# Post-LayerNorm shift (x += ab) as an accumulating DMA instead of a VectorE add, in a four-layer hybrid diffusion step

## The chip, the cores and the metric

The kernel runs on one core of one Trainium2 chip. The metric is the device time of one execution in microseconds. All matrix work is done by TensorE (PE). VectorE (DVE), ScalarE (ACT) and GpSimd (POOL) prepare operands, empty PSUM and normalise. SyncE (SP) and GpSimd issue the transfers, which all run on the same 16 DMA engines.

## The reference

640 tokens (128 of context, 512 latent) of width 1024 pass through four layers. A layer has a token mixer (gated linear attention, Conformer convolution, short convolution, and attention again) and a squared-ReLU MLP. After each of these eight sublayers the residual stream is normalised and the next one reads a modulated copy:

```python
xs = layer_norm(ALPHA * xs + ms[2] * os_, ln_g[l, 0], ln_b[l, 0])
fs = sqrelu_mlp(modulate(xs, ms[3], ms[4]), ff_w1[l], ff_w2[l])
xs = layer_norm(ALPHA * xs + ms[5] * fs, ln_g[l, 1], ln_b[l, 1])
```

`layer_norm` is (x − mean) / std · g + b. What is stored for the next residual addition is ALPHA times that, so the kernel keeps x · (ALPHA·g) + (ALPHA·b).

## The kernel before

The residual stream stays in SBUF as five tiles `x[t]` of 128 tokens by 1024 values in fp32. Every fp32 product is made of three matmuls: each weight tile of 512 KB is loaded by SP into one of 5 buffers `st`, cast by ScalarE to `whi` (L107), and VectorE makes the rest `wlo` (L108); 6 buffers of each hold weights ahead of PE. PSUM gives the mixers' and the MLP's products five banks, two named `mm` and three named `mx` (`bank`). PE needs a free bank for each pass, and ScalarE or VectorE frees one by copying it out.

`mm1` makes products with weights stationary. Of the first four weights it runs the left 384 columns first and then the right 256 columns one by one. After each it calls `evac`, which in the MLP is two ReLUs out of PSUM on ScalarE (L1159, L1160), a square on VectorE (L1162), a cast on ScalarE (L1163) and a subtraction on VectorE (L1164). Then it runs one entry of the list `self.later`. `mm2` makes the products that go back to the residual stream.

The last `mm2` of a sublayer ends in `norm_epi`, which calls `ln` for each token tile: statistics, normalisation in place, and 6.2 us of matmul time later `rest`, which transposes x, modulates it into `hT` (the operand of the next sublayer, L397 and L398) and puts the closure `affine` on `self.later`. `affine` is the stored g and b: x is multiplied by `ag` and `ab` (named `abr` in the trace) is added. Neither is needed until the next sublayer's residual addition (L205), tens of microseconds later. `issue_after(self.mark.ins)` holds the two behind the latest `hT` on VectorE's queue.

There are seven such groups of five tiles, one behind every sublayer but the last: in the trace their first multiplications start at 391.9 (in the MLP of layer 0), 856.9 (Conformer), 1099.5 (MLP of layer 1), 1565.1 (short convolution), 1793.4 (MLP of layer 2), 2283.9 (attention of layer 3) and 2585.2 us (MLP of layer 3).

`ag` and `ab` have one buffer each. After the group is done `load_ln` loads the next norm's vectors into them on GpSimd's DMA queue (L371), and ScalarE multiplies them by ALPHA in place (L373), except for the last norm. In the attention layers other tiles (`za`, `wgb`) take over the buffers (`lower`, L575).

The order of PE's instructions is that of the program (`manual_schedule`). The other engines' queues are ordered at build time by a planner with its own costs (`schedule_with_timeline_sim=True`). On the chip each queue runs strictly in that order, and an instruction that waits holds up all behind it on its engine.

Of the kernel before, what the change touches and what calls it, by code (L numbers as in the profile page):

```python
# [11 lines left out]
AL = mybir.AluOpType  # L12
# [54 lines left out]
class Net:  # L67
# [352 lines left out]
    def ln(self, t, nxt, last):  # L420
        nc, x = self.nc, self.x[t]
        mv = self.stats(x[:, :512], x[:, 512:], LN_EPS)
        if not last:
            nc.vector.tensor_scalar(
                out=x[:, :512], in0=x[:, :512], scalar1=mv[:, 0:1], scalar2=mv[:, 3:4], op0=AL.subtract, op1=AL.mult)
            nc.scalar.activation(x[:, 512:], x[:, 512:], AF.Identity, bias=mv[:, 4:5], scale=mv[:, 3:4])
            ag, ab = self.ag, self.ab

            def affine():
                with self.tc.issue_after(self.mark.ins):  # L430
                    nc.vector.tensor_tensor(out=x, in0=x, in1=ag, op=AL.mult)
                    nc.vector.tensor_tensor(out=x, in0=x, in1=ab, op=AL.add)

            def rest():
                self.modulated(t, nxt)
                self.later.append(affine)

            self.after(LN_GAP, rest)
            return
        dst = self.out["y_prompt"] if t == 0 else self.out["y_sample"][(t - 1) * 128:t * 128, :]  # L440
        for n in range(2):
            c = slice(n * 512, (n + 1) * 512)
            nc.scalar.activation(x[:, c], x[:, c], AF.Identity, bias=mv[:, 4:5], scale=mv[:, 3:4])
            nc.vector.tensor_tensor(out=x[:, c], in0=x[:, c], in1=self.ag[:, c], op=AL.mult)
            nc.vector.tensor_tensor(out=x[:, c], in0=x[:, c], in1=self.ab[:, c], op=AL.add)
            nc.sync.dma_start(dst[:, c], x[:, c])
# [853 lines left out]
```

## Time and profile before

| | |
|---|---|
| median of 3 runs | 3029.47 us (3028.68 to 3032.02) |
| profiled execution | 3029.77 us, of it the span from first to last instruction 3028.0 us |
| busy, share of the span | PE 98%, VectorE 61%, ScalarE 33%, GpSimd 5% |
| DMA | 350.28 MB, mean 116 GB/s |
| mean granted TensorE clock | 0.995 of full speed |

The profiled execution lies 0.3 us above the median. The 1.8 us between its time and its span lie outside the instructions.

### The profile page before, as it was taken

How to read it: one execution, taken by the hardware profiler on the slowest of the kernel's cores; microseconds unless marked ns; L12 is line 12 of the kernel's file. 1: busy time of each engine (PE TensorE's matmuls, PEld its weight loads, DVE VectorE, ACT ScalarE, POOL GpSimd, SP SyncE). 2: the span in 40 equal slices, each digit the busy share in tenths (PEclk: the TensorE clock that was granted, in tenths of full speed). 3: DMA queues.
4: the chain of work that ended last, by engine and by line, in shares of the span. 5: the costliest groups of instructions: out<-in, count | busy, mean ns of one | idle time of the engine just before them, and what ended most of it. 6: DMA issues, size and time to landing. Idle time of an engine off the chain costs nothing.

```text
span 3028.0 us, 42170 instructions
## 1 busy us (share of the span) xinstructions
PE 2978.6 (98%) x17452; PEld 2620.9 (87%) x17452; DVE 1850.4 (61%) x2737; ACT 999.6 (33%) x1592; POOL 154.5 (5%) x295
## 2 busy tenths in 40 slices
PE   7999999999999899999999999999999999999998
PEld 5888798898888697988999988988988887998997
DVE  4444877767597775775484486774465448644345
ACT  4333442232242341332242142322344434322221
POOL 0000100000010010000010010000010001000000
PEclk9999999999999999999999999999999999999999
DMA  6334244445165334452232133541223212322120
GB/s 247 121 122 157 87 140 150 151 151 173 65 177 135 114 110 156 162 169 93 83 112 77 63 112 112 174 164 67 82 70 121 105 63 86 107 87 73 63 91 36
DMA packets 101792, 350.28 MB, mean 116 GB/s; under 512 B 12940, under 2 KB 18572, under 8 KB 101600
## 3 DMA queue, kind: packets, MB, share of 16 engines
q1 hardware_dynamic: 91888, 317.79, 31.6%
q0 software_dynamic: 9712, 29.80, 3.0%
q8 instruction: 137, 2.24, 0.3%
q14 instruction: 55, 0.45, 0.0%
HBM read 340.29 MB, written 7.24 MB: 115 GB/s over the span
## 4 chain that ended last, share of the span: by engine, by line
PE 95%; DMA 2%; DVE 1%; ACT 1%; issue 1%; POOL 0%; SPq 0%; DVEq 0%; ACTq 0%; POOLq 0%
PE mx L143 23%; PE mm L189 22%; PE mx L189 20%; PE mm L143 19%; PE md L273 1%; PE md L338 1%; PE mx L1004 1%; PE tp L408 1%; PE o L798 1%; PE tp L778 1%; PE tp L725 1%; PE o L764 1%; DMA st<-in_gvr 1%; PE tp L748 1%; PE mm L1004 1%
## 5 line engine op out<-in xcount | busy, mean ns | idle before, releaser
L107 ACT CAST whi<-st 128x1024 fp32r<-128x1024 f32 (+1 forms) x378 | 396.0, 1050 | 1099.0 <-PE mx L189 290.7
L143 PE MATMUL mx<-hT,whi 128*128 128x256 f32 (+1 forms) x3216 | 706.9, 310 | 1.7 <-DVE hT L398 1.5
L108 DVE TENSOR_TENSOR wlo<-st,whi 128x1024 fp32r<-128x1024 f32 (+1 forms) x378 | 459.9, 1221 | 373.7 <-ACT whi L107 368.1
L143 PE MATMUL mm<-hT,whi 128*128 128x384 f32 (+1 forms) x2592 | 566.4, 309 | 1.1 <-DVE hT L398 0.8
L143 PEld LDWEIGHTS mx<-hT,whi 128*128 128x128 f32 x3216 | 541.9, 189 | 5.9 <-DVE hT L398 3.0
L143 PE MATMUL mx<-hT,wlo 128*128 128x384 f32 (+1 forms) x1608 | 497.8, 310 | 0.0
L189 PE MATMUL mx<-whi,act 128*128 128x512 f32 (+1 forms) x1536 | 484.7, 389 | 0.0
L143 PEld LDWEIGHTS mm<-hT,whi 128*128 128x128 f32 x2592 | 434.0, 189 | 5.0 <-DVE hT L398 1.7
L143 PE MATMUL mm<-hT,wlo 128*128 128x256 f32 (+1 forms) x1296 | 399.7, 308 | 0.4 <-DVE wlo L108 0.4
L189 PEld LDWEIGHTS mx<-whi,act 128*128 128x128 f32 x1536 | 287.9, 188 | 61.1 <-issue 1.7
L189 PE MATMUL mm<-whi,act 128*128 128x512 f32 (+1 forms) x1040 | 330.2, 388 | 0.0
L143 PEld LDWEIGHTS mx<-hT,wlo 128*128 128x128 f32 x1608 | 304.4, 189 | 2.5 <-issue 2.5
L189 PE MATMUL mx<-wlo,act 128*128 128x512 f32 (+1 forms) x768 | 299.2, 390 | 0.0
L320 DVE SCALAR_TENSOR_TENSOR acc<-st,cm,acc 128x512 f32<-128x512 f32 x392 | 275.9, 745 | 34.3 <-ACT acc L318 34.0
L189 PE MATMUL mm<-whi,hT 128*128 128x512 f32 x888 | 286.1, 395 | 0.0
L143 PEld LDWEIGHTS mm<-hT,wlo 128*128 128x128 f32 x1296 | 245.2, 189 | 7.8 <-issue 6.7
L189 PEld LDWEIGHTS mm<-whi,act 128*128 128x128 f32 x1040 | 194.8, 188 | 41.2 <-issue 1.7
L189 PE MATMUL mm<-wlo,act 128*128 128x512 f32 (+1 forms) x520 | 202.3, 389 | 0.0
L189 PEld LDWEIGHTS mm<-whi,hT 128*128 128x128 f32 x888 | 165.5, 188 | 31.9
L204 DVE TENSOR_TENSOR mx<-mx,gate 128x512 f32<-128x512 f32 x120 | 83.5, 696 | 162.5 <-PE mx L189 162.3
L189 PE MATMUL mm<-wlo,hT 128*128 128x512 f32 x444 | 177.3, 399 | 0.0
L189 PEld LDWEIGHTS mx<-wlo,act 128*128 128x128 f32 x768 | 144.3, 188 | 36.3 <-issue 7.5
(250 smaller groups left out, 3158.1 us busy)
## 6 DMA issues: line engine op xcount, KB each, us to landing
st<-in_w SPq DMA_DIRECT2D x256, 512.0 KB, 3.6
st<-in_modv SPq DMA_DIRECT2D x112, 512.0 KB, 4.1
st<-in_modw SPq DMA_DIRECT2D x80, 512.0 KB, 4.5
st<-in_gvr SPq DMA_DIRECT2D x32, 512.0 KB, 5.4
st<-in_cpw SPq DMA_DIRECT2D x24, 512.0 KB, 4.8
st<-in_scin SPq DMA_DIRECT2D x24, 512.0 KB, 3.5
ur<-uscr SPq DMA_DIRECT2D x40, 238.0 KB, 5.8
st<-in_gqk SPq DMA_DIRECT2D x16, 512.0 KB, 5.4
```

What stands on the lines that cost most here:

```text
L107: self.nc.scalar.copy(hi[:, :n], src)
L108: self.nc.vector.tensor_tensor(out=lo[:, :n], in0=src, in1=hi[:, :n].bitcast(F32), op=AL.subtract)
L143: self.nc.tensor.matmul(ps[:m, :n], w[a][:, kt * m:(kt + 1) * m], self.hT[:, h, kt, c0:c0 + n], start=(i == 0), stop=(i == 3 * KT - 1),)
L189: self.nc.tensor.matmul(ps, lhs(kt, h, t), s[a][:, c + cols.start:c + cols.stop], start=(i == 0), stop=(i == 3 * nk - 1))
L204: self.nc.vector.tensor_tensor(out=ps, in0=ps, in1=g, op=AL.mult)
L273: nc.tensor.matmul(ps[32 * t:32 * t + 32, :], self.cm[:, kt, :], st[t // 2][:, c:c + 512], start=(kt == 0), stop=(kt == KT - 1),)
L320: nc.vector.scalar_tensor_tensor(out=acc[:, s], in0=w, scalar=c, in1=acc[:, s], op0=AL.mult, op1=AL.add)
L338: nc.tensor.matmul(ps[r:r + 32, :], self.ones, acc[:, s], start=True, stop=True)
L408: nc.tensor.transpose(tp[:, i * 128:(i + 1) * 128], x[:, k * 128:(k + 1) * 128], self.ident)
L725: nc.tensor.matmul(sp[:, i, dd], self.tri[:, 2 + dd], G[:, t0 + i, dd], start=True, stop=True)
L748: nc.tensor.matmul(sc[:, i], Em[i][:, ts], Ep[i][:, ts], start=True, stop=True)
L1004: nc.tensor.matmul(ps[32 * g:32 * g + 32, :5 * GRID], w[:, g, q], ur[i][:, g, :, 4 * q:4 * q + GRID], start=(q == 0), stop=(q == 7))
```

## The change

In `affine` the multiplication stays on VectorE. The addition becomes a DMA that GpSimd issues: it reads the 512 KB of `ab` and accumulates them into `x` in SBUF. It stands outside the `issue_after` block. The program is otherwise the same, and the planner orders the queues anew.

```diff
             def affine():
                 with self.tc.issue_after(self.mark.ins):
                     nc.vector.tensor_tensor(out=x, in0=x, in1=ag, op=AL.mult)
-                    nc.vector.tensor_tensor(out=x, in0=x, in1=ab, op=AL.add)
+                nc.gpsimd.dma_start(x, ab, accum_op=AL.add)
```

## Rows read from the trace of the kernel before

**Rows 1.** The page's head and part 1: busy time, share of the span, instructions.

```profile
span 3028.0 us, 42170 instructions
...
PE 2978.6 (98%) x17452; PEld 2620.9 (87%) x17452; DVE 1850.4 (61%) x2737; ACT 999.6 (33%) x1592; POOL 154.5 (5%) x295
```

**Rows 2.** PE's waits from 60 us on: us in total, times, longest.

```profile
PE mm L1004 <- DMA ur<-uscr: 3.7, 1, 3.7
...
PE mm L143 <- ACT r L1160: 0.4, 1, 0.4
PE mx L143 <- ACT r L1159: 0.2, 1, 0.2
```

**Rows 3.** VectorE's groups of instructions: busy us, mean ns, idle before.

```profile
L432 DVE TENSOR_TENSOR x<-x,abr 128x1024 f32<-128x1024 f32 x35 | 40.5, 1217 | 0.0
```

**Rows 4.** Timeline of VectorE, 386 to 412 us: start, us, instruction.

```profile
391.93 5.76 DVE L431 TENSOR_TENSOR x<-x,ag 128x1024 f32<-128x1024 f32 x5
397.60 5.76 DVE L432 TENSOR_TENSOR x<-x,abr 128x1024 f32<-128x1024 f32 x5
```

**Rows 5.** Timeline of GpSimd, 386 to 412 us.

```profile
397.99 0.62 POOL L371 DMA_DIRECT2D ag<-in_ln_g  x1 [13.54 <-DVE x L431]
403.67 0.53 POOL L371 DMA_DIRECT2D abr<-in_ln_b  x1 [5.06 <-DVE x L432]
```

**Rows 6.** Timeline of ScalarE, 386 to 412 us.

```profile
408.10 1.06 ACT L373 ACTIVATE abr<-abr 128x1024 f32<-128x1024 f32 x1
...
409.68 0.48 ACT L1159 ACTIVATE r<-mx 128x384 f32<-128x384 f32 x1
```

**Rows 7.** Timeline of PE, 408 to 412 us.

```profile
410.22 0.62 PE L143 MATMUL mx<-hT,whi 128*128 128x384 f32 x2 [0.18 <-ACT r L1159]
```

**Rows 8.** DMA issues of the whole span: KB each, median us to landing.

```profile
ur<-uscr SPq DMA_DIRECT2D x40, 238.0 KB, 5.8
...
gate<-gate POOLq DMA_DIRECT2D x16, 512.0 KB, 4.5
...
abr<-in_ln_b POOLq DMA_DIRECT2D x8, 512.0 KB, 4.5
...
gate<-gate POOLq DMA_DIRECT2D x4, 256.0 KB, 3.5
```

**Rows 9.** Timelines of ScalarE in three other groups.

```profile
875.04 1.06 ACT L373 ACTIVATE abr<-abr 128x1024 f32<-128x1024 f32 x1 [1.74 <-DMA abr<-in_ln_b]
...
879.09 0.59 ACT L962 ACTIVATE u<-mx,prm 128x384 f32<-128x384 f32 x1 [2.04 <-PE mx L143]
...
1581.80 1.06 ACT L373 ACTIVATE abr<-abr 128x1024 f32<-128x1024 f32 x1 [0.81 <-DMA abr<-in_ln_b]
...
1589.86 1.05 ACT L107 CAST whi<-st 128x1024 fp32r<-128x1024 f32 x1 [3.16 <-PE mm L143]
...
1809.48 1.05 ACT L373 ACTIVATE abr<-abr 128x1024 f32<-128x1024 f32 x1
```

**Rows 10.** Windows: stretch, busy us of each engine, PE clock, DMA share, GB/s.

```profile
391.00:404.00 13.00, 13.00 (x92) 13.00 (x90) 12.79 (x13) 2.57 (x4) 0.96 (x2) 1.00 0.27 100
...
870.00:890.00 20.00, 20.00 (x157) 19.31 (x159) 16.47 (x20) 7.06 (x13) 0.55 (x1) 1.00 1.00 262
2283.00:2298.00 15.00, 15.00 (x87) 12.61 (x89) 15.00 (x19) 1.99 (x5) 0.00 (x0) 1.00 0.00 0
```

**Rows 11.** Timelines of GpSimd, SP and PE, first convolution of the Conformer.

```profile
870.67 0.55 POOL L985 DMA_DIRECT2D uscr<-u  x1 [0.99 <-DVE u L964]
...
877.75 3.67 SPq L997 DMA_DIRECT2D ur<-uscr  x8
...
888.83 4.51 PE L1004 MATMUL mm<-ur,st 128*32 128x320 f32 x64
```

**Rows 12.** Timeline of ScalarE, attention of layer 3.

```profile
2297.97 0.72 ACT L575 CAST za<-low 98x640 fp32r<-98x640 f32 x1 [7.57 <-DVE x L432]
...
2310.62 1.04 ACT L107 CAST whi<-st 128x1024 fp32r<-128x1024 f32 x1 [8.80 <-DMA st<-in_gqk]
```

## The prediction

> **What bounds the kernel now.** I read the page's busy times first. PE is busy for 2978.6 of 3028.0 us [rows 1], so whatever is taken from another engine is worth only the part of PE's idle time that it ends. Next I read what PE waits for once the opening is past. There are 14 entries between 3.7 us and 0.2 us, and they add up to 22.9 us [rows 2]. Only two of them stand behind an affine group, both of them waits for ScalarE to empty a PSUM bank, 0.4 and 0.2 us. The largest, 3.7 us, is a convolution's transfer 100 us after the nearest group. VectorE is busy for 61%, so its time in the sum bounds nothing.
>
> Then I read the group itself, in the MLP of layer 0. Five multiplications run from 391.93 us, and five additions from 397.60 us to 403.36 us, without a gap [rows 4]. The reader is to see what hangs on their ends. The load of the next `ag` is issued 0.3 us after the last multiplication, that of the next `abr` at 403.67 us, 0.3 us after the last addition [rows 5]. ScalarE scales `abr` at 408.10 us [rows 6], 4.43 us after that issue, as long as such a load takes to land [rows 8]. It stands in the middle of ScalarE's queue: the next PSUM copy (L1159) comes at 409.68 us [rows 6], and PE is already waiting for it at 410.22 us, for 0.18 us [rows 7]. So a chain with no slack leads from the last addition through a transfer and ScalarE to PE. It is hidden only because each piece ends just in time.
>
> **What the change takes away.** 35 additions of 1217 ns, 40.5 us of VectorE [rows 3]. VectorE gets free 5.7 us earlier in each group and squares the ReLUs sooner, which can end the two small waits, 0.6 us in all [rows 2]. I count −0.6 us. No multiplication moves, since each stays behind the same `hT`.
>
> **What it adds on GpSimd.** 35 issues at about the 0.53 us of the `abr` load [rows 5], 19 us on an engine that is busy for 5% [rows 1]. Each waits for one multiplication, and these end 1.14 us apart, so in a group GpSimd is held for about 6 us. In that stretch it otherwise stands waiting for the same multiplications (13.54 us before `ag` [rows 5]). I cost the issues at nothing. Behind them stand the loads of `ag` and `abr`, and in the Conformer the copy `uscr` at 870.67 us [rows 11]. What that costs is priced below.
>
> **What it adds in the wait for `abr`.** The buffer is free when five accumulating transfers have landed, not when five additions have ended. No transfer into SBUF with arithmetic is in the trace, so I bound it. From GpSimd's queue 512 KB land in 4.5 us and 256 KB in 3.5 us [rows 8]. Worked out from these, 512 KB more cost 2.0 us and a transfer's fixed part is 2.5 us. The first accumulate can be issued at 391.93 + 1.22 + 0.3 = 393.4 us.
> - Lower bound: it costs as much as a copy. The last one lands at 393.4 + 2.5 + 5 × 2.0 = 405.9 us, `abr` is issued at 406.2 and scaled at 410.6 us. That is 2.5 us later than now.
> - Upper bound from rows: it reads `x` as well as `ab`, so its traffic counts twice, 4.0 us each. The last one lands at 415.9 us, and `abr` is scaled 12.5 us late.
> - I take 2.7 us each, a third of the way up: the writing is that of a copy and only the reading doubles. Last landing 409.4 us, `abr` scaled 6.0 us late.
>
> The DMA engines themselves have room there: their share is 0.27 from 391 to 404 us [rows 10].
>
> The Trainium skill (DMA: Bandwidth & Descriptors, Rules for kernel authors) says that an accumulating DMA reads its destination and writes it later. No run here shows that yet. By it the upper bound would be the nearer one.
>
> **What this costs on PE, group by group.** If ScalarE keeps its order, all behind the scaling moves by the same delay.
> - MLP of layers 0, 1 and 2: PE has no slack there [rows 7], and the order around 1809.48 us is the same [rows 9]. 3 × 6.0 = 18 us (bounds 7.5 and 37.5).
> - Conformer: two paths, of which the longer counts. After the scaling at 875.04 us ScalarE idles 2.04 us before the next bank's copy [rows 9], and one bank's pass of 2.6 to 3.8 us (24 matmuls of 256 or 384 columns at the 0.11 and 0.16 us that the kernel's own beat gives them) covers more: 6.0 − 2.0 − 3 = 1 us. The other path is on GpSimd, where the load of `abr` stands ahead of `uscr` at 870.67 us. Behind that come `ur` on SP, from 877.75 to 881.42 us, and the convolution at 888.83 us [rows 11]. The four `ur` for its first half are issued by some 879.6 us and land 5.8 us later in the median [rows 8], so 3.5 us are to spare: 6.0 − 3.5 = 2.5 us (bounds 0 and 9). DMA is full from 870 to 890 us [rows 10], so what slips into that stretch isn't made up there.
> - Short convolution: after 1581.80 us there is no idle time on ScalarE until 3.16 us at 1589.86 us [rows 9]. 6.0 − 3.5 = 2.5 us, the bank's pass taken off (bounds 0 and 8).
> - Attention of layer 3: ScalarE's copy `za` waits for the last addition until 2297.97 us [rows 12]. DMA is empty there [rows 10]. By the middle price the accumulates land at 2283.89 + 1.5 + 2.5 + 13.5 = 2301.4 us, 3.4 us later. ScalarE then idles 8.80 us before 2310.62 us for a weight [rows 12], which takes it up: 0 us (bounds 0 and 1.3).
> - MLP of layer 3: `abr` isn't scaled by ScalarE for the last norm and is needed only at the end. 0 us.
> - Weights: 2.6 MB more per group delay the `st` loads, but six cast weights stand ahead of PE, each good for some 6 us of matmuls. 0 us.
>
> Sum: −0.6 + 18 + 2.5 + 2.5 = 22.4 us. The profiled execution's 3029.8 us become 3052.2 us. The median lies 0.3 us lower, so I say 3052. The bounds give −0.6 + 7.5 = 6.9 us (3036) and −0.6 + 37.5 + 9 + 8 + 1.3 = 55.2 us (3085).
>
> **Rivals.**
> 1. *No change, about 3029.* Two ways lead there. The planner may price the accumulate as long as it really is, and set the scaling of `ab` so much later in ScalarE's queue that its load has landed. What is behind then doesn't wait, and `ab` isn't needed for hundreds of us. Against that: now it stands exactly at the landing (a wait of 1.74, 0.81 and 0 us [rows 9]), so its costs fit ordinary loads. It is unknown whether they fit an accumulate. Or the accumulate is quicker than the rows let me think: it decides at the point where the fifth lands by 403.4 us, 10.0 us after the first issue, as the additions end now. Each would have to take 1.5 us, 350 GB/s. Chance 0.34 together. The Trainium skill's fit for a GpSimd-issued transfer (DMA: Bandwidth & Descriptors, Anatomy of one DMA) is 2.0 us plus bytes over 436 GB/s. By it five land after an estimated 8.0 us, and this rival comes true.
> 2. *An accumulate far slower than twice a copy.* At 8 us each the fifth lands at 435.9 us and the scaling is 32.5 us late: 3 × 32.5 + 29 + 29 + 21 (attention, where its 8.80 us of idle time and some 3 us more cover part) = 176 us, about 3206. Nothing in the trace speaks for it, and nothing excludes it. Chance 0.08.
> 3. *Faster, about 3020.* VectorE's 40.5 us come off and the new order happens to end the convolution's wait of 3.7 us and its neighbours. By more than 6 us it must end over a quarter of all the 22.9 us of waits, of which 0.6 us touch the groups. Chance 0.06.
>
> **How the numbers follow.** My forecast (slower by 7 to 55 us) has 0.52, rival 1 0.34, rival 2 0.08, rival 3 0.06. About 0.2%, 6 us, is what a measurement of this kernel tells from no change. Slower: 0.52 + 0.08 = 0.60. Same: 0.34. Faster: 0.06. The forecast's own range is 3036 to 3085. The range for 8 in 10 takes in rival 1 and goes a little past the upper bound: 3026 to 3100.
>
> **What would show it.** In the changed trace `abr` is loaded more than 10 us after the last multiplication, ScalarE's L373 waits some 6 us for `DMA abr`, and PE waits about as long for ScalarE's L1159 or L1160 in three MLPs. VectorE loses 40.5 us of busy time, and GpSimd's queue carries 18 MB more. The forecast is wrong if L373 stands later in ScalarE's queue and waits for nothing, if the fifth accumulate lands within 10 us of the first issue, or if PE's new waits lie elsewhere, at `ur` or at `wlo`.

## The result, and the profile after

| | before | after |
|---|---|---|
| median beside each other, 4 runs each | 3029.07 us | 3055.03 us (3051.50 to 3055.41) |
| ratio, 95% interval | | 1.0082 [1.0064, 1.0099] |
| profiled execution, its span | 3029.77, 3028.0 us | 3051.50, 3049.7 us |

The change costs 26 us. The profiled execution is the quickest of the four, 3.5 us below the median, so its rows explain a little less than the whole. Its busy times, with the line of the software-issued DMA queue (packets, MB, share of the 16 engines' span):

```profile
span 3049.7 us, 42242 instructions
...
PE 2984.9 (98%) x17452; PEld 2626.7 (86%) x17452; DVE 1810.8 (59%) x2702; ACT 997.6 (33%) x1592; POOL 181.6 (6%) x330
...
q0 software_dynamic: 14752, 48.15, 6.2%
```

VectorE lost 39.6 us of work [rows 1], as the diff promises, and nothing came of it. PE executes the same 17452 matmuls and is busy 6.3 us longer for them. That part of the loss can't be a wait; it is a lower clock in places. The waits of PE from 60 us on (total, times, longest) show the larger part:

```profile
PE mx L143 <- ACT r L1159: 9.0, 2, 6.4
PE mm L143 <- ACT r L1160: 7.1, 1, 7.1
PE mm L1004 <- DMA ur<-uscr: 6.7, 2, 3.8
```

All 14 entries add up to 38.7 us, before to 22.9. The two waits for ScalarE's PSUM copies were 0.2 and 0.4 us [rows 2] and are now 16.1 us in three places, one in each MLP of layers 0, 1 and 2. The convolution's wait for `ur` was 3.7 us, once; a second one of 2.9 us is new.

I also set the start of each matmul after against that of the same matmul before. The lag grows in four places and almost nowhere else:

| | lag before it | lag behind it |
|---|---|---|
| MLP of layer 0 | −2.2 us | +6.2 us |
| Conformer | +5.8 | +9.4 |
| MLP of layer 1 | +9.4 | +12.3 |
| short convolution | +12.3 | +12.1 |
| MLP of layer 2 | +12.1 | +20.9 |
| attention and MLP of layer 3 | +20.9 | +20.5 |

The −2.2 us is there by 250 us, before the first accumulate is issued. It is no gain of the change.

Now the group in the MLP of layer 0, queue by queue. First GpSimd: of the five accumulates the first and the last, then the two loads.

```profile
391.52 0.96 POOL L432 DMA_DIRECT2D x<-abr  x1 [9.28 <-issue]
...
396.12 0.86 POOL L432 DMA_DIRECT2D x<-abr  x1 [0.34 <-issue]
396.65 0.88 POOL L371 DMA_DIRECT2D ag<-in_ln_g  x1
408.89 0.54 POOL L371 DMA_DIRECT2D abr<-in_ln_b  x1 [11.36 <-issue]
```

By the trace the five land at 396.11, 398.85, 401.54, 404.02 and 408.24 us, the fifth 16.7 us after the first issue. The load of `ag` is issued right behind the fifth, at 396.65 us. It needs only the multiplications, which are over. But it lands at 411.17 us, 2.9 us behind the fifth accumulate and 14.5 us after its issue. In each of the six groups that load an `ag`, it lands 2.5 to 4.7 us behind the fifth accumulate. The DMA issues of the whole span (KB, median us to landing) show the size; the load of `ag` took 4.1 us before:

```profile
x<-abr POOLq DMA_DIRECT2D x35, 512.0 KB, 7.8
...
ag<-in_ln_g POOLq DMA_DIRECT2D x8, 512.0 KB, 14.2
abr<-in_ln_b POOLq DMA_DIRECT2D x8, 512.0 KB, 5.0
```

ScalarE in the same stretch:

```profile
403.23 0.72 ACT L1163 CAST act<-r 128x640 fp32r<-128x640 f32 x1
411.19 1.06 ACT L373 ACTIVATE ag<-ag 128x1024 f32<-128x1024 f32 x1 [7.24 <-DMA ag<-in_ln_g]
412.15 1.03 ACT L107 CAST whi<-st 128x1024 fp32r<-128x1024 f32 x1
413.09 0.72 ACT L1163 CAST act<-r 128x640 fp32r<-128x640 f32 x1
413.71 0.48 ACT L1159 ACTIVATE r<-mx 128x384 f32<-128x384 f32 x1
414.10 0.37 ACT L1160 ACTIVATE r<-mm 128x256 f32<-128x256 f32 x1
414.36 1.05 ACT L373 ACTIVATE abr<-abr 128x1024 f32<-128x1024 f32 x1
```

The reader is to see one instruction that waits 7.24 us for a landing, and the copy out of PSUM that stands three places behind it (413.71 us). Before, that copy came at 409.68 us [rows 6], and PE ran 2.2 us later there, so the copy is 6.2 us late. The scaling of `abr`, on which the prediction looked, comes 0.5 us after its load has landed and waits for nothing. PE stops 3.9 us after ScalarE does, and restarts with the copy:

```profile
407.56 0.28 PE L143 MATMUL mx<-hT,wlo 128*128 128x256 f32 x1
414.25 1.01 PE L143 MATMUL mx<-hT,whi 128*128 128x384 f32 x2 [6.41 <-ACT r L1159]
415.06 0.52 PE L143 MATMUL mx<-hT,wlo 128*128 128x384 f32 x1
```

Two of these matmuls take 1.01 us where before two took 0.62 [rows 7]. The windows say why (busy us of each engine; the last three columns are PE's granted clock, DMA share, GB/s; the first four windows are layer 0, the fifth and sixth layer 1, the last two layer 2):

```profile
400.00:408.00 8.00, 7.84 (x66) 7.64 (x64) 4.66 (x5) 2.40 (x5) 0.00 (x0) 1.00 1.04 222
408.00:414.20 6.20, 0.00 (x0) 0.00 (x0) 0.99 (x1) 3.01 (x5) 0.54 (x1) 0.84 0.69 246
414.20:418.00 3.80, 3.75 (x12) 3.75 (x13) 3.33 (x5) 3.80 (x7) 0.00 (x0) 0.50 0.40 138
418.00:422.00 4.00, 4.00 (x25) 4.00 (x24) 4.00 (x7) 1.57 (x3) 0.00 (x0) 0.87 0.71 231
...
1131.00:1134.00 3.00, 0.42 (x3) 0.19 (x2) 1.22 (x2) 3.00 (x6) 0.00 (x0) 1.00 0.20 60
1134.00:1138.00 4.00, 4.00 (x31) 4.00 (x31) 3.53 (x6) 3.25 (x7) 0.00 (x0) 1.00 0.45 134
1823.00:1830.30 7.30, 0.19 (x2) 0.00 (x0) 1.28 (x2) 3.31 (x6) 0.54 (x1) 0.66 0.59 225
1830.30:1834.00 3.70, 3.68 (x11) 3.68 (x12) 3.23 (x5) 3.70 (x7) 0.00 (x0) 0.50 0.43 142
```

After waits of 6.4 and 7.1 us PE restarts at 0.50 of full speed, the 1.2 GHz level. The lag grows by 2.2 and 2.4 us more while that lasts, from 4.0 to 6.2 us and from 18.5 to 20.9 us. After the wait of 2.6 us in layer 1 the clock stays at 1.00 in this execution.

In the Conformer the delay reaches PE by way of GpSimd, SP and the convolution. The three timelines:

```profile
883.83 0.55 POOL L371 DMA_DIRECT2D abr<-in_ln_b  x1 [13.40 <-DMA x<-abr]
884.36 0.55 POOL L985 DMA_DIRECT2D uscr<-u  x1
...
889.67 3.91 SPq L997 DMA_DIRECT2D ur<-uscr  x8
...
897.61 5.85 PE L1004 MATMUL mm<-ur,st 128*32 128x320 f32 x64 [2.87 <-DMA ur<-uscr]
```

GpSimd stands 13.40 us before the load of `abr`, until the fifth accumulate has landed. `uscr`, next in its queue, is issued at 884.36 us; before it was 870.67 us [rows 11]. PE lost 2.9 us to the wait. Behind it the lag grows on to 10.1 us at a lower clock, 0.66 granted from 897 to 902 us; 0.7 us of that is gone again at 1119 us, so that 3.6 us remain.

### The profile page after: what moved, and what is told of

It is laid out like the page before. It is cut to its first block, busy times and chain, and to the rows that moved or that the text cites. A ratio compares the mean times of both kernels' runs of the same rounds, so it can differ in the third digit from the quotient of the medians.

```text
span 3049.7 us, 42242 instructions
## 1 busy us (share of the span) xinstructions
PE 2984.9 (98%) x17452; PEld 2626.7 (86%) x17452; DVE 1810.8 (59%) x2702; ACT 997.6 (33%) x1592; POOL 181.6 (6%) x330
## 3 DMA queue, kind: packets, MB, share of 16 engines
HBM read 340.29 MB, written 7.24 MB: 114 GB/s over the span
## 4 chain that ended last, share of the span: by engine, by line
PE 60%; DMA 1%; DVE 1%; ACT 1%; issue 0%; POOL 0%; DVEq 0%; ACTq 0%; POOLq 0%
PE mx L143 16%; PE mx L189 14%; PE mm L189 14%; PE mm L143 12%; PE md L338 1%; PE tp L778 0%; PE tp L408 0%; PE o L798 0%; DMA ag<-in_ln_g 0%; PE pa L143 0%; PE md L273 0%; PE tp L725 0%; PE o L764 0%; PE tp L748 0%; PE tp L705 0%
```

## The experiments

The theory: the five accumulates land later than the order of the queues allows for, and an in-order engine waits for them at a place that PE needs. The rivals: it is only the place of `ag` in the software queue (first experiment); it is the DMA traffic or GpSimd's work itself (third); the loss depends on a fixed time of the accumulates and not on their bytes (last).

**`ag` loaded by SP, the other queue.**

```diff
         for dst, src in ((self.ag, "ln_g"), (self.ab, "ln_b")):
-            nc.gpsimd.dma_start(dst, self.d[src][l, i:i + 1, :].broadcast_to([128, 1024]))
+            (nc.sync if src == "ln_g" else nc.gpsimd).dma_start(dst, self.d[src][l, i:i + 1, :].broadcast_to([128, 1024]))
```

> The load of ag is issued from SP's hardware queue, so it no longer stands behind the five accumulates on GpSimd's software queue. Theory (the loads behind the accumulates hold up ScalarE): ag lands within 6 us of the last multiplication and ScalarE's 7.2 us wait for it goes, but the load of abr must still wait until the fifth accumulate has landed, so ScalarE now waits 3 to 7 us for abr, and PE waits 2 to 6 us in each of three MLPs: 3036 to 3050 us. Rival 1 (the place behind the accumulates in one queue is all of the cost): abr's scaling finds its load landed and the time is 3029 to 3034. Rival 2 (the accumulates slow PE's other supplies by their traffic): unchanged, 3052 to 3058.

Measured: 3047.16 us (3042.40 to 3052.59, 5 runs), ratio 1.0049 [1.0036, 1.0062]. About 9 of the 26 us are gone, 17 are left, inside the theory's range. The profiled execution is 4.8 us quicker than this median, so its rows show less than the whole. ScalarE in the MLP of layer 0 now waits at both scalings:

```profile
406.59 1.06 ACT L373 ACTIVATE ag<-ag 128x1024 f32<-128x1024 f32 x1 [5.19 <-DMA ag<-in_ln_g]
...
416.81 1.06 ACT L373 ACTIVATE abr<-abr 128x1024 f32<-128x1024 f32 x1 [4.71 <-issue]
```

On SP's queue `ag` lands 10 us after its issue (396.46 to 406.51 us), not within the time that I expected; the DMA engines, which it shares with the accumulates and the weights, are full there (a share of 1.05 from 396.4 to 406.5 us). The planner also set its scaling earlier in ScalarE's queue, behind the first L1160 as in the kernel before. The fifth accumulate lands at 411.23 us, `abr` is issued at 411.80 and lands at 416.67. So the place of `ag` in the software queue isn't all of the loss, and that rival falls. How much of the 9 us is the place, and how much the new order of ScalarE's queue, isn't separated.

**The same transfers without the arithmetic.** They overwrite `x` with `ab`, so nothing is added.

```diff
-                nc.gpsimd.dma_start(x, ab, accum_op=AL.add)
+                nc.gpsimd.dma_start(x, ab)
```

> Leaves out the arithmetic: the DMA copies ab into x and adds nothing, so x is ab afterwards. Same bytes landed, same queues in the same order on every engine. Theory (an accumulate costs more per 512 KB than a copy, and that excess times five is part of the wait): landings of one group 2.0 us apart instead of 2.6, ag lands some 11 us after its issue instead of 14.2, PE's waits for ScalarE in the MLPs shrink by some 3 us each, 16.1 us to 6 to 9 in all, time 3038 to 3047. Rival (an accumulate moves at a copy's rate, only the queue counts): landings stay 2.6 us apart and the time 3052 to 3058.

Measured: 3028.06 us (3026.15 to 3031.22, 11 runs), ratio 0.9992 [0.9983, 1.0001]. The whole loss is gone, more than I expected. All five engines' queues stand in the same order as after the change. So the new order by itself costs nothing: with real copies it fits. That the planner takes an accumulate to be as long as a copy is inferred from the equal order; its costs weren't read. On the page, the line of the software queue and that of the 35 transfers:

```profile
q0 software_dynamic: 14752, 48.15, 4.6%
...
x<-abr POOLq DMA_DIRECT2D x35, 512.0 KB, 3.7
```

The timelines of GpSimd (first and fifth copy) and ScalarE in the MLP of layer 0:

```profile
392.56 0.62 POOL L432 DMA_DIRECT2D x<-abr  x1 [9.27 <-issue]
...
397.17 0.53 POOL L432 DMA_DIRECT2D x<-abr  x1 [0.67 <-DVE x L431]
...
404.88 1.06 ACT L373 ACTIVATE ag<-ag 128x1024 f32<-128x1024 f32 x1
```

The five copies land at 395.50, 396.89, 398.41, 399.70 and 401.79 us: the fifth comes 9.2 us after the first issue, against 16.7. `ag` lands at 403.73 and is scaled at 404.88 us, without a wait. The same packets and bytes take 4.6% of the DMA engines' span here and 6.2% as accumulates; before it was 3.0%. So 35 copies cost 1.6% of 3025 us, 1.4 us of all 16 engines each, and 35 accumulates 3.2% of 3050 us, 2.8 us each. An accumulate takes twice a copy's time on the DMA engines.

**The accumulates stay, the scaling stands later.** ScalarE's two scalings are held behind the last cast of the block of products, in the Conformer behind a late sigmoid. In the Conformer the two loads are also held, on GpSimd's queue, behind an `uscr` copy. In the MLP (the short convolution is alike):

```diff
-                    nc.scalar.copy(a[:, 0], r)
+                    self.hold = nc.scalar.copy(a[:, 0], r)
...
-                    self.load_ln(l, 1, last)
+                    with tc.issue_after(self.hold.ins):
+                        self.load_ln(l, 1, last)
```

> The accumulates stay; ScalarE's two scalings of ag and abr are held behind its last cast of the same block of products (MLP, short convolution) or a late sigmoid (Conformer), and in the Conformer the two loads are held behind an early uscr copy. Theory: ScalarE no longer waits in front of PSUM copies, PE's 16.1 us of waits for L1159 and L1160 go, and with them the stretches at the lower clock, and the Conformer's wait for ur falls below 2 us: 3026 to 3034 us. Rival (traffic of the accumulates, or GpSimd's issues, hold up PE): 3045 to 3056.

Measured: 3029.64 us (11 runs), ratio 0.9994 [0.9985, 1.0003]. In the MLP of layer 0 ScalarE scales `ag` without a wait, 33 us later than after the change:

```profile
444.05 1.05 ACT L373 ACTIVATE ag<-ag 128x1024 f32<-128x1024 f32 x1
```

Among PE's waits none for a ReLU on ScalarE is left, and the largest is again that of before:

```profile
PE mm L1004 <- DMA ur<-uscr: 3.7, 1, 3.7
```

The window in which PE stood idle is full:

```profile
408.00:414.00 6.00, 6.00 (x47) 6.00 (x47) 5.63 (x7) 3.78 (x6) 0.55 (x1) 1.00 1.01 269
```

The traffic of the accumulates is all there (DMA share 1.01), and so is GpSimd's work: 181.6 us as after the change. Neither costs anything that these runs can tell. The loss is the wait in ScalarE's and GpSimd's queues, and the rival of traffic falls.

**The same hold on the kernel before**, as a control.

> The kernel before (additions on VectorE) with the same hold on the scalings, as a control. Theory: the scalings there cost 0.6 us of PE's waits at most, so 3026 to 3031 us, no change that can be told. If the hold is worth something by itself, it is faster by over 4 us, and what the fourth experiment's other kernel gains must be reduced by that.

Measured: 3030.83 us (11 runs), ratio 0.9999 [0.9990, 1.0008]. The hold by itself brings nothing that can be told, so what it gives back above is what the accumulates had cost. It also shows that the offload gains nothing even when it is arranged well: 3029.64 against 3030.83 us, inside both intervals.

**Accumulates in three MLPs only, and in the other four groups only.** The other groups add on VectorE. The flag is set in the loop over the layers, for the first kernel `False` before a mixer and `not last` before an MLP, for the second `True` and `last`:

```diff
+                    if not self.by_dma:
+                        nc.vector.tensor_tensor(out=x, in0=x, in1=ab, op=AL.add)
-                nc.gpsimd.dma_start(x, ab, accum_op=AL.add)
+                if self.by_dma:
+                    nc.gpsimd.dma_start(x, ab, accum_op=AL.add)
```

> Only the groups in the MLPs of layers 0, 1 and 2 accumulate by DMA; the other four add on VectorE. Theory (the cost is ScalarE's wait in these three, 8.5 + 2.6 + 8.9 us of shift with the lower clock after it): 3046 to 3053 us, 17 to 23 slower than before. Rival (the cost is spread over all seven groups, by traffic): three sevenths of 26 us, 3040.

> Only the other four groups (Conformer, short convolution, attention of layer 3, MLP of layer 3) accumulate by DMA. Theory: only the Conformer costs, by the late uscr and ur, 3.5 us of shift: 3030 to 3036 us. Rival (spread over all groups): four sevenths of 26 us, 3044.

Measured: the three MLPs 3054.13 us (5 runs), ratio 1.0075 [1.0063, 1.0088]; the other four 3038.33 us (8 runs), ratio 1.0028 [1.0017, 1.0038]. They lie 1 and 2 us above what I had expected at most. Waits of PE in the first (its lines stand 3 lower in the file, so that L1162 and L1163 are the two ReLUs):

```profile
PE mx L143 <- ACT r L1162: 8.5, 2, 6.0
PE mm L143 <- ACT r L1163: 6.8, 1, 6.8
```

The three MLPs carry most of the loss. In layer 1 PE again waits about as long as after the change, 2.5 us, but this time the granted clock falls to 0.50 from 1134.9 to 1138.3 us.

The parts, 24.0 and 8.2 us, add up to 32, more than the 26 of the whole. Each kernel has a new order of queues, and in each the lag behind the kernel before grows by some 3 us at one place of the attention of layer 3, more than 500 us after the accumulates before it: around 2398 us in the first, 2262 us in the second. At both the granted clock is 0.50, for 6.8 and 3.4 us. The two places together are about the excess of 6 us. What sets them off isn't settled, so the parts are good to a few us only.

**Half the columns.** VectorE adds the right 512 columns, the DMA the left ones.

```diff
+                    nc.vector.tensor_tensor(out=x[:, 512:], in0=x[:, 512:], in1=ab[:, 512:], op=AL.add)
-                nc.gpsimd.dma_start(x, ab, accum_op=AL.add)
+                nc.gpsimd.dma_start(x[:, :512], ab[:, :512], accum_op=AL.add)
```

> Only the left 512 of 1024 columns are added by the accumulating DMA, 256 KB each; VectorE adds the right half. Theory (2.6 us for each 512 KB accumulate, five behind one another, against additions that the planner's order is fitted to): 1.3 us each, so the five land within some 11 us of the first issue instead of 16.7, ag lands 8 to 10 us after its issue, and ScalarE's waits in the MLPs fall below 3 us each, PE's below 1: 3027 to 3036 us. Rival (an accumulate costs a fixed time whatever its size): landings stay 2.6 us apart and the time 3048 to 3057.

Measured: 3040.14 us (3034.37 to 3044.46, 10 runs), ratio 1.0036 [1.0026, 1.0046], between both expectations. The profiled execution is 4.1 us quicker than this median, so its rows again show less than the whole; the six runs over 3040 us have a mean granted clock of 0.993 or 0.994, the other four of 0.995. In the MLP of layer 0 the transfers did what the theory says: they land 1.3 to 2.1 us apart, the fifth 9.7 us after the first issue. But the time didn't follow. ScalarE in the MLP of layer 0:

```profile
405.01 1.06 ACT L373 ACTIVATE ag<-ag 128x1024 f32<-128x1024 f32 x1 [2.83 <-DMA ag<-in_ln_g]
...
409.16 1.06 ACT L373 ACTIVATE abr<-abr 128x1024 f32<-128x1024 f32 x1 [1.25 <-DMA abr<-in_ln_b]
```

The waits of PE (lines stand 1 lower, so L1160 and L1161 are the ReLUs):

```profile
PE mm L143 <- ACT r L1161: 3.4, 1, 3.4
PE mx L143 <- ACT r L1160: 1.7, 1, 1.7
```

The planner moved as well: it set the scaling of `ag` three instructions earlier than after the change, behind the first L1160 of the kernel before. `ag` lands at 404.93 us, 1.2 us later than with full copies (in an execution whose group starts 0.7 us later). ScalarE waits for it here and didn't there. So the transfer's time alone doesn't decide. What counts is how far the landing lies behind the place that the queue's order gives the waiting instruction.

## Why the prediction was right, and where not

The forecast of 3052 us lies 3 us below the measured median, and the mechanism is the one forecast: accumulates land later than additions end, a load behind them is late, ScalarE waits at its scaling, and PE waits for ScalarE. By its steps:

- **VectorE, −0.6 us.** The multiplications stay together and 39.6 us of work are gone. The two small waits of before are swallowed by the new ones, so the 0.6 us can't be seen. In the two kernels without the loss nothing above the scatter appears.
- **Price of an accumulate: 2.7 us forecast, 2.5 to 2.7 us between the first four landings in the MLP of layer 0.** The first step to it was off and the second made up for it, which is luck: a copy was put at 2.0 us, and by the DMA engines' time it takes 1.4; the accumulate is then twice a copy (2.8), as in my upper bound, and not a third of the way to it. The fifth came 4.2 us behind the fourth, and landed 16.7 us after the first issue, 16.0 forecast. The Trainium skill (DMA: Bandwidth & Descriptors, Rules for kernel authors) has the accumulate read its destination and write it later, and the doubled time of the packets agrees with that in direction. By its fit for one transfer (Anatomy of one DMA) five would have landed after an estimated 8.0 us; the copies took 9.2 us, paced by multiplications 1.14 us apart, and the accumulates 16.7 us, so the fit doesn't hold for them.
- **Which wait.** The prediction named the load of `abr`, and had it wrong. The load of `ag`, whose buffer is free early, stands behind the accumulates on the same queue and lands behind them: 14.2 us after its issue in the median, 4.1 before. I had counted "the loads of `ag` and `abr`" as standing behind the issues on GpSimd, and priced only the second. ScalarE's wait of 7.24 us is for `ag`; `abr` then waits for nothing. The size came out right all the same, 6.2 us in the MLP of layer 0 against 6.0, but by luck: `ag` lands 2.9 us behind the fifth accumulate, where `abr` lands 5.6 us behind it, and its scaling stands three places ahead of PE's copy instead of two.
- **What the planner does** was rival 1 in part. It moved the scaling of `ag` from behind the first L1160 to behind the next L1163, room enough for copies. The order is the same in the kernel with copies, which waits for nothing. The rival needed an order that fits the accumulate, and the planner's fits the copy. Its dividing point, the fifth landing within 10.0 us of the first issue, is none: with half columns that took 9.7 us, and 10.7 us were lost.
- **MLPs, 18 us forecast, 20.1 measured** (8.4, 2.9 and 8.8). Not 6.0 three times: new waits of 6.2, 2.6 and 6.8 us, and 2.2 and 2.4 us of lower clock in layers 0 and 2, which the prediction didn't have. That layer 1 has as little slack as the other two was taken for granted, not read. There PE ran on for 8.0 us after ScalarE stopped, and for 3.9 us in layer 0.
- **Conformer, 2.5 us forecast, 3.6 measured,** by the path through `uscr` and `ur`, as forecast: the `ur` transfers are issued 6.1 us late, the lag of 5.8 us before them taken off, and PE waits for 2.9 us, so 3.2 us were to spare, where the prediction had 6.0 and 3.5. The lower clock adds 0.7.
- **Short convolution, 2.5 us forecast, none measured.** ScalarE waits 7.99 us for `ag` at 1598.02 us there, and the profile shows no wait of PE from 1575 to 1615 us. So the slack, put at 3.5 us, is the term that was too small; how PE's banks cover the wait wasn't traced. (By its own terms the upper bound is 12.5 − 3.5 = 9 us and not 8.)
- **Attention and MLP of layer 3, 0 us:** so it was. ScalarE's `za` waits 7.7 us for the last accumulate, and PE isn't held up.
- **GpSimd's issues at nothing:** right, though the row of an accumulate on GpSimd is 0.86 us long and not 0.53. The kernel with late scaling has the same issues and no loss.

That the total is so close is luck, since the steps that were off nearly cancel: MLPs +2.1 and Conformer +1.1 more than forecast, short convolution 2.5 less, and an opening 2.2 us earlier in the profiled execution. The 3.5 us by which the other three runs are longer than the profiled one aren't explained by its trace.

## What to carry to other kernels

Work taken from an engine that doesn't set the end may be worth nothing, and it can cost what the new carrier delays: here 40 us less on VectorE gained nothing in the best order tried and cost 26 us in the planner's. When an instruction is replaced by a DMA, follow what stands behind it on the DMA's own queue as well as what waits for its data. Where the queues are planned ahead, set an instruction that waits for a new or unpriced transfer behind the work that the bounding engine needs (here holding two instructions of ScalarE, and two loads in the Conformer, gave the 26 us back). Don't count on a smaller transfer to mend it: the plan moved with it here, and half the bytes still cost 10.7 us.

## What the runs showed of the hardware that was not expected

- In the attention of layer 3, where the DMA engines had a share of 0.04 before (2283 to 2306 us) and 0.95 with them, the five accumulates of 512 KB within SBUF landed 2.5 to 2.7 us apart. In the other six groups, beside other transfers, it was 2.3 to 4.2 us, with 3.4 us or more for the fifth; around the 4.2 us of the MLP of layer 0 the DMA share was 1.04. In that MLP accumulates of 256 KB and copies of 512 KB landed 1.3 to 2.1 us apart, both issued 1.1 to 1.2 us apart. In time of the 16 DMA engines it is 2.8 us for an accumulate and 1.4 us for a copy, both of 512 KB.
- The row of an accumulate's issue on GpSimd is 0.86 us long, that of the copy's 0.53 us. The next issue starts 0.53 us after the fifth accumulate's all the same (396.12 and 396.65 us), and the plain load of `ag` there has 0.88 us, against 0.54 us behind copies. So the row's length need not be the time for which the queue is held.
- A load issued behind five accumulates on the same queue landed 2.9 us after the last of them in the MLP of layer 0. From SP's queue the same load still took 10 us.
- PE came back at the 1.2 GHz level after standing idle for 6.4 and 7.1 us and lost 2.2 and 2.4 us more. For short waits the runs show both: after 2.6 us idle in the MLP of layer 1 the granted clock was 1.00 throughout, after 2.5 us at the same place in the kernel with three MLPs it fell to 0.50 for 3.4 us, and around the 2.9 us idle in the Conformer it was 0.50 for 3.4 us.
